# The z gates of both mixers by one Silu instead of halved product, Tanh and second product

## The chip, the cores and the metric

The kernel runs on one core of one Trainium2 chip. The metric is the device time of one execution in microseconds; the time given for a kernel is the median of its runs. The engines are called as in the profile: PE (matrix products), DVE and POOL (elementwise work), ACT (activation functions, copies, casts), SP (issues most transfers).

## The reference

One inference step of a two-layer decoder trunk for 512 prompt tokens and 8 sample tokens, which share weights; the kernel holds them side by side as 520 columns. Layer 0 is a hybrid mixer (window attention beside a Mamba-2 scan), layer 1 a gated delta net; a SwiGLU feed-forward layer follows each. In both mixers the input projection also gives a gate z, and the mixer's output is multiplied by silu(z) = z * sigmoid(z):

```python
# layer 0
y = (y + d_skip[:, None] * xs).reshape(bsz, L, SSM_D_INNER) * silu(z)
y = y * rsqrt(mean(y * y) + EPS)          # per group of 512 features
# layer 1
o = rmsnorm(o, norm_w) * silu(z.reshape(bsz, L, GDN_V_HEADS, GDN_DV))
```

The gate has 1024 features in layer 0 and 2048 in layer 1.

## The kernel before, in words

All activations lie feature-major: a tile is 128 features on the partitions by 520 token columns, which are worked in two halves of 256 and 264 columns (`HALF`). A linear layer (`lin`, line 299) holds the weights still and moves the tokens: each weight tile is split on chip into a rounded part `whi` (a cast on ACT, or on DVE) and a remainder `wlo` (a subtraction on POOL or DVE, line 165), and three products per weight tile go into a PSUM buffer `acc` for each half. There are four `acc` buffers, so two tiles of 128 features can stand in PSUM; PE cannot start a third until DVE has read the first.

The per-token norm of the layer's input is applied behind the product: the row `R2` of 520 factors multiplies the PSUM result. So a z gate needs z = acc * R2 and then silu(z). With silu(z) = (z/2) * (1 + tanh(z/2)), the kernel does this by three instructions for each half:

- a `scalar_tensor_tensor` on DVE (helper `stt`, shown as line 281): half = acc * 0.5 * R2, which also frees PSUM;
- a Tanh on ACT (helper `act`, line 284) into a scratch tile;
- a second `scalar_tensor_tensor` on DVE (line 281): (tanh + 1) * half.

Scratch comes from `tmp` (line 240), a ring of three buffers with the name `sq`, which other steps use as well.

Layer 0 (`gate_z`, line 558, called at line 649): eight z tiles, in two groups of four. The result `zt` lies in a `b` buffer (shown as `p`), and only the tanh lies in `sq`: the second product reads as `p<-sq,p`. `l0_gate` (line 861) then multiplies by the scan's output (`p<-p` or `p<-b,p`, 520 columns) and adds squares for the group's norm; `l0_norm` (line 867) takes Ln and Exp for each half, normalises and splits the result into the operands of the output projection. Ahead of that in program order are the attention of the prompt (`l0_attn`, line 936: scores, a maximum on DVE, an Exp on ACT shown as `p<-p,ast`, a reciprocal, a scaling on POOL, transposes) and of the samples (`l0_attn_sample`, line 991: eight products on POOL with the reductions of line 1011 on DVE, one Exp, then small transfers through DRAM called `pd`).

Layer 1 (`l1_gate`, line 1667, called at line 1305): sixteen z tiles. Here both the half product and the tanh lie in the `sq` ring: the second product reads as `sq<-sq`. A third product with the norm weight and the delta rule's output follows (`sq<-sq,par,Hh` or `sq<-sq,par,p`), then a cast on ACT, and a subtraction for the remainder. After the first eight tiles comes `l1_sample_state` (line 1822): for 16 pieces of the samples' states it loads a state `Hh` and a row set `ud` into one of two `cs` buffers, scales the state on POOL or DVE, adds on DVE by four `scalar_tensor_tensor` (`Hh<-cs,CS,Hh`), and stores the state. `l1_sample_gate` (line 1810) makes the sample columns of the output projection's operands (`X<-CS,p`); PE cannot finish the first tile of the output projection (`out_proj`, line 469) before.

Ahead of both gates the convolutions (`conv_tile`, line 518) also use Tanh, and the feed-forward layers use Silu already (line 1097), there with a data product on DVE ahead, a plain `tensor_tensor` (helper `tt`, shown as line 274).

The order of the instructions on each engine is laid out when the kernel is built, by a planner that takes instructions by priority (program order, or early where `high_priority` stands) as they come ready by its own durations. So work of later program lines fills gaps of earlier ones: the z tiles of layer 0 are spread among the attention's items, and the sample states of layer 1 among its z tiles. Each engine then works through its list in order. Before an activation whose function is not in the active table an ACT_TABLE_LOAD is put in; it appears in the profile under the line of the activation.

Of the kernel before, what the change touches and what calls it, by code (L numbers as in the profile page):

```python
# [121 lines left out]
def KN(n, v, *others):  # L122
    """The engine, share or order chosen at a place: v unless the table has another of the choices."""
    return KNOBS.get(n, v)
# [4 lines left out]
class WStream:  # L129
    """Weights, in the order of use: loaded in groups, split into hi + lo in units of at most 4 row tiles."""  # L130
# [38 lines left out]
    def tile(s, ap, c0, kts, spread=None, ncol=None, out=None):  # L169
        """Yield (row tile, hi, lo) for the 128 columns from c0 and the row tiles kts; input weights come two tiles a load.  # L170
        out = (buffer, offset) of 1024 floats for each four row tiles, to hold them apart from the ring."""
# [12 lines left out]
    def rows(s, ap, c0, loads):  # L184
        """As tile() for a tall matrix; loads are (first row tile, count, unit offsets in their order)."""
        for k0, n, offs in loads:
            raw = s.load(ap, k0, n, c0, 128)
            for o in offs:
                m = min(4, n - o)
                hi, lo = s.split(raw, o, m, 0)  # L190
                for j in range(m):
                    yield k0 + o + j, hi[:, j], lo[:, j]


class Ker:
# [14 lines left out]
    def gen(s, *names):  # L210
        """From here on these buffers hold something else: float32r operands and float32 data never share a tile."""
# [3 lines left out]
    def lay(s, name, off=0, n=KD, dt=F32R):  # L215
        """Operand (tile, half) -> columns, for n tiles of all tokens."""
# [3 lines left out]
    def layh(s, name, n=KD):  # L220
        """As lay(), the first half of the tokens of every tile before the second."""
        return lambda k, h: s.B(name, 256 * n * h + k * HW[h], HW[h], dt=F32R)
# [63 lines left out]
    def cp(s, e, out, in_):  # L286
        """Copy on ACT, DVE or GpSimd."""
# [10 lines left out]
    # ---- linear layers: weights stationary, 520 token columns moving in two halves  # L298
    def lin(s, w, xh, xl, nkt, halves=(0, 1), ps=None):
        """ps[half] = sum over row tiles of w (yielding (row tile, hi, lo)) of hi'xh + hi'xl + lo'xh."""  # L300
# [7 lines left out]
    def group(s, w, xh, xl, nkt):  # L308
        """Up to four tiles, the first half of the tokens of all before the second half, which may come later."""
# [13 lines left out]
    def lnexp(s, ins):  # L323
        """After ins, one table load for Ln and Exp."""
# [3 lines left out]
    def rstd(s, out, ps, n, e=EPS, keep=None, after=None):  # L328
        """out = rsqrt(ps / n + e), refined by a Newton step; keep = EPS * (ps / n + e)."""
# [17 lines left out]
    # ---- setup  # L347
# [66 lines left out]
    def add_sq(s, h, x, first, tmp, eng=None):  # L414
        """accT += x^2."""
# [7 lines left out]
    def prenorm(s, n, l, hi, lo, h, upd=None):  # L423
        """hi + lo = x * gain, exactly split."""
# [9 lines left out]
    def token_norm(s, h, keep=None):  # L434
        """s.R2 = per-token rsqrt(mean x^2 + eps), on every partition."""
# [7 lines left out]
    def boundary(s, deferred):  # L443
        """x += mp * rsqrt(mean m^2 + eps), then the next layer's prenorm (n, l, hi, lo): the second half, and the norms."""
# [5 lines left out]
    def residual(s, deferred, h):  # L450
        """One half's update of x, as a function of the feature tile."""
# [17 lines left out]
    def out_proj(s, rows, xh, xl, nkt, mp, n, l, pre, tail=2, final=False):  # L469
        """mp = m * gain, accT + sqs = sum m^2 for the eight tiles of an output projection; the last ones by token halves."""  # L470
# [46 lines left out]
    # ---- causal convolution of one 128-feature tile, then silu  # L517
# [26 lines left out]
    def conv_sample(s, nt, new, old, w, bias, out, tmp):  # L544
        """new [128, nt, 8], old [128, nt, 8, 3], w(j) [128, nt]; out [128, nt, 8] = silu(conv)."""
# [12 lines left out]
    def gate_z(s, ps, zt):  # L558
        """zt = silu(z)."""
        for h in (0, 1):  # L560
            zh = zt[:, HALF[h]]
            with s.tc.high_priority():
                s.stt(zh, ps[h], 0.5, s.R2[:, HALF[h]], ALU.mult, ALU.mult)
            tz = s.tmp(HW[h])
            s.act(tz, zh, AF.Tanh)
            s.stt(zh, tz, 1.0, zh, ALU.add, ALU.mult)

    def softplus(s, out, x, n):
        """out = max(x, 0) + log1p(exp(-|x|)); log1p(e) = 2 atanh(e / (2 + e)) as a series. Shapes [128, n]."""
# [16 lines left out]
    # ---- layer 0: input projection and mixers in the order of issue  # L586
# [78 lines left out]
    # ---- layer 0: sample convolution state  # L665
# [21 lines left out]
    # ---- layer 0: dt, decays in token layout  # L687
# [53 lines left out]
    # ---- layer 0: SSD over four chunks of 128 tokens, for one group of heads  # L741
# [78 lines left out]
    # ---- layer 0: one SSM step per sample  # L820
# [39 lines left out]
    # ---- layer 0: gate, grouped norm  # L860
# [6 lines left out]
    def l0_norm(s, g, zt, yh, yl):  # L867
        """y * silu(z) (in zt), normalised, to the exactly split yh + yl."""
# [11 lines left out]
    # ---- layer 0: attention of the prompt  # L880
# [25 lines left out]
    def l0_tokens(s, hp):  # L906
        """Keys and values token-major: the caches of the prompt and of the samples, V for the products."""
# [82 lines left out]
    # ---- layer 0: attention of the samples over their cached rows  # L990
# [67 lines left out]
    # ---- SwiGLU  # L1058
# [55 lines left out]
    def cache_shift(s):  # L1114
        """The samples' rolling caches: all rows but the oldest move up by one."""
# [11 lines left out]
    def final_early(s):  # L1127
        """x and the norm's eps of the second half token-major."""
# [27 lines left out]
    def final_first(s):  # L1156
        """The first half's outputs; m of the second half token-major, as far as it is known."""
# [26 lines left out]
    def final_last(s):  # L1184
        """The second half's outputs, token-major: x + m * rsqrt(mean m^2 + eps)."""
# [19 lines left out]
    # ---- layer 1: gated delta net, input projection and mixer in the order of issue  # L1205
# [119 lines left out]
    def vo(s, g, h, j):  # L1325
        """Half h of the tokens of v head 8 g + j: V token-major, then the outputs feature-major."""
# [5 lines left out]
    # ---- layer 1: beta, decays in token layout  # L1332
# [553 lines left out]
```

## Time and profile before

| | before |
|---|---|
| median of 3 runs | 1905.85 us |
| lowest and highest run | 1904.42, 1915.31 us |
| span of the profiled execution | 1901.6 us |
| mean granted clock of PE | 0.965 |
| z stage of layer 0 | about 263 to 364 us of the span |
| z stage of layer 1 | about 1270 to 1389 us of the span |

The profiled execution's own time is known as its span, from its first to its last instruction; the runs lie about 4 us above it. In the profile a group of instructions is shown as line, engine, operation, written tile and read tiles, shapes and count; behind the bar come the busy time in us, the mean in ns of one, and the idle time of the engine just ahead of them with what ended it. A row of the order in time is start, duration, engine, line, operation, count, and in brackets the idle time ahead. In the table by stage, each engine's busy time is followed by its count of instructions, then come the granted clock of PE, the busy share of the transfer engines and GB/s. The chain of waits is followed back from the last instruction, at each step to what released it.

### The profile page before, as it was taken

How to read it: one execution, taken by the hardware profiler on the slowest of the kernel's cores; microseconds unless marked ns; L12 is line 12 of the kernel's file. 1: busy time of each engine (PE TensorE's matmuls, PEld its weight loads, DVE VectorE, ACT ScalarE, POOL GpSimd, SP SyncE). 2: the span in 40 equal slices, each digit the busy share in tenths (PEclk: the TensorE clock that was granted, in tenths of full speed). 3: DMA queues.
4: the chain of work that ended last, by engine and by line, in shares of the span. 5: the costliest groups of instructions: out<-in, count | busy, mean ns of one | idle time of the engine just before them, and what ended most of it. 6: DMA issues, size and time to landing. Idle time of an engine off the chain costs nothing.

```text
span 1901.6 us, 36269 instructions
## 1 busy us (share of the span) xinstructions
PE 1746.8 (92%) x14263; PEld 1659.2 (87%) x14263; DVE 1190.0 (63%) x2334; ACT 748.7 (39%) x1828; POOL 876.2 (46%) x768
## 2 busy tenths in 40 slices
PE   8899999898999999988968898989889999999996
PEld 7888777698999999977857787978889899999996
DVE  6898878638323221178899977888954954443125
ACT  5432335555222223355756555544334511111222
POOL 2565756234444433435474554646668411112452
PEclk9999999998999999999988899999989899999998
DMA  7345765453333334453442123257998333432333
GB/s 259 125 130 183 237 202 142 145 182 113 111 111 112 112 106 136 124 177 114 137 139 72 59 65 92 63 156 212 272 290 237 132 135 134 134 133 84 92 92 106
DMA packets 293323, 268.88 MB, mean 141 GB/s; under 512 B 11841, under 2 KB 276742, under 8 KB 291986
## 3 DMA queue, kind: packets, MB, share of 16 engines
q1 hardware_dynamic: 292502, 265.90, 45.5%
q8 instruction: 112, 1.84, 0.4%
q10 hardware_dynamic: 652, 0.68, 0.1%
q14 instruction: 57, 0.47, 0.1%
HBM read 241.01 MB, written 62.04 MB: 159 GB/s over the span
## 4 chain that ended last, share of the span: by engine, by line
PE 56%; DVE 26%; DMA 8%; issue 4%; ACT 4%; POOL 2%; SPq 1%; DVEq 0%; POOLq 0%; ACTq 0%
PE acc L268 48%; DVE p L274 4%; DVE cs L281 4%; PE ma L268 4%; PE mb L268 3%; DVE b L274 2%; DVE sq L281 2%; DMA raw<-in_w_ffn_down_dram 2%; DVE p L281 1%; DVE Hh L281 1%; PE mb L271 1%; DVE cs L274 1%; DMA bm<-csd 1%; POOL cs L274 1%; DVE wlo L165 1%
## 5 line engine op out<-in xcount | busy, mean ns | idle before, releaser
L165 POOL TENSOR_TENSOR wlo<-raw,whi 128x512 fp32r<-128x512 f32 (+3 forms) x373 | 500.8, 1346 | 676.7 <-ACT whi L289 368.1
L268 PE MATMUL acc<-Hl,whi 128*128 128x256 f32 (+1 forms) x2576 | 565.6, 291 | 20.2 <-DVE Hl L281 8.5
L268 PEld LDWEIGHTS acc<-Hl,whi 128*128 128x128 f32 x2576 | 420.5, 193 | 35.4 <-issue 11.3
L289 ACT CAST whi<-raw 128x512 fp32r<-128x512 f32 (+3 forms) x392 | 234.4, 602 | 453.0 <-PE acc L268 388.2
L268 PE MATMUL acc<-Hh,whi 128*128 128x256 f32 (+1 forms) x1824 | 387.0, 287 | 3.5 <-DVE cs L274 2.0
L268 PE MATMUL acc<-Hh,wlo 128*128 128x256 f32 (+1 forms) x1824 | 389.0, 288 | 0.0
L268 PEld LDWEIGHTS acc<-Hh,whi 128*128 128x128 f32 x1824 | 292.5, 191 | 8.2 <-issue 5.1
L268 PEld LDWEIGHTS acc<-Hh,wlo 128*128 128x128 f32 x1824 | 292.8, 191 | 7.5 <-issue 6.7
L268 PE MATMUL acc<-bm,whi 128*128 128x256 f32 (+1 forms) x1136 | 237.1, 290 | 1.4 <-DVE bm L281 1.4
L268 PE MATMUL acc<-p,whi 128*128 128x264 f32 (+1 forms) x1280 | 230.6, 287 | 4.4 <-ACT p L1819 1.6
L290 DVE CAST whi<-raw 128x512 fp32r<-128x512 f32 x131 | 61.1, 467 | 256.7 <-PE acc L268 195.2
L165 DVE TENSOR_TENSOR wlo<-raw,whi 128x512 fp32r<-128x512 f32 (+1 forms) x150 | 117.5, 785 | 142.2 <-ACT whi L289 138.8
L268 PEld LDWEIGHTS acc<-p,whi 128*128 128x128 f32 x1280 | 190.6, 192 | 6.4 <-ACT p L1819 1.9
L268 PEld LDWEIGHTS acc<-bm,whi 128*128 128x128 f32 x1136 | 182.1, 193 | 3.7 <-issue 1.6
L268 PE MATMUL acc<-p,wlo 128*128 128x256 f32 (+1 forms) x704 | 164.4, 288 | 8.7 <-DVE wlo L165 7.0
L268 PE MATMUL acc<-Hl,wlo 128*128 128x256 f32 (+1 forms) x752 | 171.1, 293 | 1.0 <-POOL wlo L165 0.9
L268 PEld LDWEIGHTS acc<-Hl,wlo 128*128 128x128 f32 x752 | 126.4, 195 | 3.2 <-POOL wlo L165 1.6
L268 PEld LDWEIGHTS acc<-p,wlo 128*128 128x128 f32 x704 | 119.6, 192 | 10.1 <-DVE wlo L165 7.9
L281 DVE SCALAR_TENSOR_TENSOR cs<-cs,cw 128x512 f32<-128x512 f32 x100 | 96.4, 966 | 12.7 <-POOL cs L274 8.6
L268 PE MATMUL acc<-X,whi 128*128 128x264 f32 (+1 forms) x512 | 100.4, 291 | 1.7 <-DVE X L274 1.3
L268 PEld LDWEIGHTS acc<-X,whi 128*128 128x128 f32 x512 | 80.4, 195 | 3.2 <-DVE X L274 1.6
L281 DVE SCALAR_TENSOR_TENSOR Hh<-cs,CS,Hh 128x256 f32<-128x256 f32 x64 | 53.1, 894 | 26.5 <-POOL Hh L274 26.2
(465 smaller groups left out, 2932.6 us busy)
## 6 DMA issues: line engine op xcount, KB each, us to landing
raw<-in_w_gdn_in_dram SPq DMA_DIRECT2D x24, 1024.0 KB
raw<-in_w_ffn_gate_dram SPq DMA_DIRECT2D x22, 1024.0 KB
raw<-in_w_ffn_up_dram SPq DMA_DIRECT2D x22, 1024.0 KB
raw<-in_w_ffn_down_dram SPq DMA_DIRECT2D x20, 1024.0 KB
raw<-in_w_hyb_in_dram SPq DMA_DIRECT2D x16, 1024.0 KB
out_sv_dram<-in_cache_attn_v_dram SPq DMA_DIRECT2D x16, 1023.0 KB
out_sk_dram<-in_cache_attn_k_dram SPq DMA_DIRECT2D x16, 1023.0 KB
raw<-in_w_gdn_out_dram SPq DMA_DIRECT2D x10, 1024.0 KB
```

Source lines behind the costliest of these rows:

```text
L165: eng.tensor_tensor(out=lo[:, :nk, d:d + n], in0=raw[:, :, o:o + n], in1=hi[:, :nk, d:d + n].bitcast(F32), op=ALU.subtract)
L268: s.nc.tensor.matmul(out, lhsT=lhsT, rhs=rhs, start=start, stop=stop, skip_group_check=skip)
L271: s.nc.tensor.transpose(out, in_, s.ident[0:in_.shape[0], 0:in_.shape[0]])
L274: return (eng or s.nc.vector).tensor_tensor(out=out, in0=a, in1=b, op=op).ins
L281: return s.nc.vector.scalar_tensor_tensor(out=out, in0=a, scalar=sc, in1=b, op0=op0, op1=op1).ins
L289: return s.nc.scalar.copy(out, in_).ins
L290: return (s.nc.vector if e == "V" else s.nc.gpsimd).tensor_copy(out, in_).ins
```

## The change

The halving goes: DVE multiplies PSUM by `R2` alone, a Silu on ACT works in place, and the second product on DVE is not there any more. The scratch tile for the tanh goes with it, so `l1_gate` takes one buffer of the `sq` ring for a half instead of two, and `gate_z` takes none instead of one.

```diff
     def gate_z(s, ps, zt):
         for h in (0, 1):
             zh = zt[:, HALF[h]]
             with s.tc.high_priority():
-                s.stt(zh, ps[h], 0.5, s.R2[:, HALF[h]], ALU.mult, ALU.mult)
-            tz = s.tmp(HW[h])
-            s.act(tz, zh, AF.Tanh)
-            s.stt(zh, tz, 1.0, zh, ALU.add, ALU.mult)
+                s.tt(zh, ps[h], s.R2[:, HALF[h]], ALU.mult)
+            s.act(zh, zh, AF.Silu)
...
     def l1_gate(s, g, j, ps, hi, lo):
         for h in (0, 1):
             z = s.tmp(HW[h])
             with s.tc.high_priority():
-                s.stt(z, ps[h], 0.5, s.R2[:, HALF[h]], ALU.mult, ALU.mult)
-            tz = s.tmp(HW[h])
-            s.act(tz, z, AF.Tanh)
-            s.stt(z, tz, 1.0, z, ALU.add, ALU.mult)
+                s.tt(z, ps[h], s.R2[:, HALF[h]], ALU.mult)
+            s.act(z, z, AF.Silu)
```

The convolutions keep their Tanh. Comments and descriptions of functions were taken out as well, with the line numbers kept.

## Prediction

> **What bounds the kernel now.** I read the page first, for the engines' shares and the chain that ended last.
>
> ```profile
> span 1901.6 us, 36269 instructions
> PE 1746.8 (92%) x14263; PEld 1659.2 (87%) x14263; DVE 1190.0 (63%) x2334; ACT 748.7 (39%) x1828; POOL 876.2 (46%) x768
> PE 56%; DVE 26%; DMA 8%; issue 4%; ACT 4%; POOL 2%; SPq 1%; DVEq 0%; POOLq 0%; ACTq 0%
> ```
>
> PE is the bound on the whole, but a quarter of the chain is DVE's, and the change takes work from DVE. Whether it pays depends on the two places where z gates run. So I read next the table by stage: layer 0's z stage (263 to 364), its quiet middle left out, then layer 1's (1270 to 1389) in three parts.
>
> ```profile
> 263.00:328.00 65.00, 62.78 (x464) 50.87 (x463) 55.25 (x138) 32.30 (x96) 43.13 (x39) 1.00 0.63 174
> 345.00:364.00 19.00, 14.16 (x78) 9.20 (x77) 13.47 (x28) 16.14 (x31) 5.21 (x6) 0.91 0.68 226
> 1270.00:1292.00 22.00, 20.76 (x203) 15.67 (x201) 21.04 (x43) 9.52 (x23) 8.46 (x8) 1.00 0.92 259
> 1292.00:1320.00 28.00, 27.80 (x242) 24.91 (x239) 21.32 (x42) 13.33 (x28) 15.62 (x13) 1.00 0.73 211
> 1320.00:1389.00 69.00, 52.54 (x359) 49.46 (x358) 65.48 (x106) 21.68 (x52) 45.23 (x32) 0.86 0.87 247
> ```
>
> The columns are length, PE, PEld, DVE, ACT, POOL, clock, transfer share, GB/s. The last row is the one that matters: for 69 us DVE is busy 65.48 (95%) while PE has 359 products, which at the rate of the row above it (27.80 us for 242, 0.115 us each) are 41 us of work. PE is starved there, and its clock falls to 0.86. From 1292 to 1320 PE is full (27.80 of 28.00). The chain of waits inside the last part and inside layer 0's stage confirms it:
>
> ```profile
> by line: DVE sq L281 27.4%; DVE Hh L281 27.0%; DMA cs<-ud 16.9%; issue 6.7%; PE acc L268 5.6%; DVE p L274 4.4%; DVE CS L274 3.7%; DVE CS L278 3.5%; ACT p L289 1.8%; ACT sq L284 1.2%; SPq L296 1.2%; PE mb L271 0.4%; DVE X L274 0.3%; DVE acc
> ```
>
> ```profile
> by line: issue 10.4%; DVE p L281 9.7%; DMA cs<-in_state_ssm_dram 8.7%; DVE p L274 7.5%; DMA pd<-p 6.3%; DMA p<-sqd 6.1%; DVE p L1011 5.8%; PE ma L268 5.7%; POOL bm L274 4.7%; DVE wlo L165 4.4%; DVE p L957 4.1%; ACT L284 3.7%; ACT p L284 3.1
> ```
>
> In layer 1 (first row) the gate's products `sq L281` are the largest item of the chain; in layer 0 (the row below) they are about a tenth, among attention, transfers and ACT.
>
> **The change part by part.** First the product that frees PSUM. Its form changes from three operands with a constant to two operands; the feed-forward layers run the new form on the same shape.
>
> ```profile
> L281 DVE SCALAR_TENSOR_TENSOR sq<-acc,R 128x264 f32<-128x264 f32 x16 | 6.8, 424 | 0.3
> L274 DVE TENSOR_TENSOR sq<-acc,R 128x264 f32<-128x264 f32 x41 | 17.4, 423 | 0.1
> L284 ACT ACTIVATE sq<-sq 128x264 f32<-128x264 f32 x16 | 6.8, 425 | 20.0 <-DVE sq L281 19.6 <-DVE p L274 0.4
> L284 ACT ACTIVATE cs<-sq 128x264 f32<-128x264 f32 x22 | 9.3, 423 | 0.3 <-DVE sq L274 0.3
> ```
>
> 424 against 423 ns: nothing. The third row is the gate's Tanh, the fourth the feed-forward layers' Silu: 425 against 423 ns, nothing either.
>
> Second, the product (tanh + 1) * half goes: 32 instructions in layer 1, 16 in layer 0. These are its rows in layer 1 from 1320 to 1389, then in layer 0.
>
> ```profile
> L281 DVE SCALAR_TENSOR_TENSOR sq<-sq 128x264 f32<-128x264 f32 x8 | 7.3, 918 | 0.0
> L281 DVE SCALAR_TENSOR_TENSOR sq<-sq 128x256 f32<-128x256 f32 x8 | 4.2, 527 | 1.0 <-ACT sq L284 1.0
> ...
> L281 DVE SCALAR_TENSOR_TENSOR p<-sq,p 128x256 f32<-128x256 f32 x8 | 6.6, 829 | 0.0
> L281 DVE SCALAR_TENSOR_TENSOR p<-sq,p 128x264 f32<-128x264 f32 x8 | 5.6, 694 | 0.0
> ```
>
> For **layer 1's last part** that is 7.3 + 4.2 = 11.5 us off an engine that is 95% busy. The upper bound of the gain is 11.5 us, plus at most 1.0 us for the waits on ACT; the lower bound is 0, if something else holds the stretch. What is late next? PE would allow 69 - 41 = 28 us. The transfers would allow less: a share of 0.87 of 69 us is 60 us, so 9 us are left if the bytes in the stretch stay the same. Which of DVE and the transfers waits for the other is seen in SP's waits and in the sample states' row of this stretch:
>
> ```profile
> SPq L296 <- DVE Hh L281: 23.5, 6, 9.8
> ```
>
> ```profile
> L281 DVE SCALAR_TENSOR_TENSOR Hh<-cs,CS,Hh 128x256 f32<-128x256 f32 x33 | 21.4, 706 | 0.3 <-DMA cs<-ud 0.3
> ```
>
> SP waits 23.5 us for DVE to free the sample states' buffers; DVE waits 0.3 us for their rows. So the transfers follow DVE. I take 9 us, the smaller of 11.5 and the transfers' 9. In **layer 1's first parts** 16 more of these products go, but PE is busy 20.76 of 22.00 and 27.80 of 28.00 us: at most 1.4 us can come out, and I take 0.5. The smaller need of the `sq` ring (one buffer for a half instead of two) lets DVE run further ahead of ACT; its worth is inside the 1.0 us of waits above, and I take 0.
>
> For **layer 0** 6.6 + 5.6 = 12.2 us of DVE work goes, from a stretch in which DVE is busy 55.25 of 65.00 us. How much of it lies on the chain is read from the chain in order of time:
>
> ```profile
> 289.94 3.52 DVE p L281 x2
> ...
> 311.70 1.25 DVE p L281 x2
> ...
> 320.95 1.47 DVE p L281 x2
> ```
>
> These three pieces are second products: 3.52 + 1.25 + 1.47 = 6.2 us. Bounds 0 and 12.2; I take 5, as something else ready at nearly the same time will hold part of it.
>
> Third, what the change adds: **table loads on ACT**. The row of all loads at that line, then how Silu follows Exp today:
>
> ```profile
> L284 ACT ACT_TABLE_LOAD x24 | 30.8, 1283 | 7.2 <-DVE cs L281 6.0 <-DVE small L278 0.8
> ```
>
> ```profile
> 467.77 0.88 ACT L284 ACTIVATE rs<-rs 128x264 f32<-128x264 f32 x2 [0.96 <-DVE rs L278]
> 468.67 1.28 ACT L284 ACT_TABLE_LOAD   x1
> 469.96 0.42 ACT L284 ACTIVATE cs<-sq 128x256 f32<-128x256 f32 x1
> ```
>
> The pair `rs` is Ln and Exp, the last row the first Silu of the feed-forward layer: between the table with Exp used there and Silu's stands a load of 1.28 us. Tanh costs no load beside the attention's Exp: no load stands in ACT's order from 47.28 to 344.84, with both functions in use. So each change from Silu to the attention's Exp and back will cost one. ACT's order in the stage, Tanh as `sq<-p`, Exp as `p<-p,ast`, the intermediate rows left out, and as its first row the load for the convolutions' Tanh:
>
> ```profile
> 47.28 1.28 ACT L284 ACT_TABLE_LOAD   x1
> ...
> 263.40 0.77 ACT L284 ACTIVATE sq<-p 128x256 f32<-128x256 f32 x2 [1.73 <-DVE p L281]
> ...
> 273.32 0.40 ACT L284 ACTIVATE p<-p,ast 128x128 f32<-128x128 f32 x1 [3.31 <-DVE ast L278]
> ...
> 314.81 0.61 ACT L284 ACTIVATE p<-p,ast 128x384 f32<-128x384 f32 x1 [2.00 <-DVE ast L278]
> ...
> 344.84 1.28 ACT L284 ACT_TABLE_LOAD   x1
> 346.14 0.42 ACT L284 ACTIVATE rs<-rs 128x256 f32<-128x256 f32 x1
> ```
>
> The planner has spread the z tiles among the attention's items. The first six tiles each have Exps behind them before the next: six changes there and back, 12 loads; the seventh tile comes after the last Exp, one load; the eighth after the first half's Ln and Exp of the norm, one load. The loads for Ln and Exp stand there already. That is 14 loads, 14 * 1.283 = 18.0 us of ACT, which is busy 32.30 of 65.00 us in the first part. Many are covered, because a load with nothing to wait for runs while ACT idles ahead of its activation (3.31 and 2.00 us in the Exp rows above, 1.73 in the first Tanh's). What is not covered delays an Exp, and DVE's next reciprocal waits for it. Cost on the path: 0 to 18.0 us. I take two loads, 2.5 us: one before the last attention items, where z, Exp and the samples' Exp stand close together, one in the norm (345 to 364), where ACT is busy 16.14 of 19.00 us. In layer 1 the Ln and Exp of the samples' output stand between z tiles; one load for the first Silu and one behind that Exp make 2 loads, 2.6 us on an ACT busy a third of the time, covered by DVE's own work. I take 0.
>
> The Trainium skill, page "ScalarE: Activation LUTs", section "What ACT_TABLE_LOAD costs", gives 1283 ns for the load and 1380 ns for a drain with it, 2.66 us a switch. The trace has the 1283 ns, but the Ln at 346.14 starts 0.02 us after its load ends (344.84 + 1.28 = 346.12), so no drain is seen behind it. By the page, as an estimate, 16 switches would be 43 us of ACT instead of 20.5.
>
> **The sum.** -9 (layer 1's last part) - 0.5 (its first parts) - 5 + 2.5 (layer 0) = -12 us. Against the profiled span: 1901.6 - 12 = 1889.6 us. The median of the runs, 1905.85, stands 4.25 us above that span, which the change doesn't touch: 1893.9, so 1894 us, 0.6% below before.
>
> **The rivals.** *The transfers or the sample states hold layer 1.* For: the transfer share of 0.87, 16.9% of the chain there on `cs<-ud`, and the planner may put more sample states into the freed time, ahead of the output projection. Against: SP's 23.5 us of waits for DVE. Then layer 1 gives 0 and layer 0's -2.5 alone is left: 1903 us.
>
> *The table loads decide, and it becomes slower.* One mechanism, in layer 0: Silu and Exp alternate. The planner's order also may part the two halves of a tile by an Exp, which makes up to two more loads for each of seven tiles, 28 in all. Each uncovered load is 1.283 us; against them stand layer 1's 9.5 and layer 0's chain share of 6.2, so it decides from 15.7 / 1.283, 12 uncovered loads on. With 21 of 28 uncovered it is 27 - 15.7 = +11 us: 1917. For: ACT's list is in order, and DVE waits for Exp with its reciprocals. Against: ACT idles for about half of the stage, often just ahead of an Exp. The Trainium skill speaks for this rival: "ScalarE: Activation LUTs", section "Table sets: the hidden batching unit", says to batch activations by table set; by that rule 14 changes of set are the wrong trade, and the trace of before, with Tanh and Exp in one set, can't show it.
>
> *All the freed DVE time counts.* Layer 0's 12.2, layer 1's 12.5 with its waits on ACT, and 1.4 in front, no load exposed: -26 us, 1880. For: DVE pieces all along the chain, and PE's clock of 0.86, which would recover if PE were fed. Against: PE's and the transfers' own limits.
>
> *No switch at all*: the change doesn't alternate tables, because Silu stands in a set with the attention's Exp. Against: the load before the first Silu at 468.67. Then 2.5 us less: 1891.
>
> **How the numbers follow.** Forecast 0.42, transfers hold 0.20, loads decide 0.15, all counts 0.18, no switch 0.05. About 1% (19 us) is what a measurement of this kernel tells from no change. Below 1886.8 lie most of "all counts" and the edge of the forecast: 0.20. Above 1924.9 lies the far part of "loads decide": 0.07. The rest is 0.73. The forecast's own range is 1886 to 1901. The range, 1879 to 1916, takes in all the middle cases, and leaves out about half of "all counts" below and half of "loads decide" above.
>
> **What would show it.** DVE's count falls by 48, and rows `sq<-sq` and `p<-sq,p` of line 281 vanish. ACT_TABLE_LOAD rises by about 16, nearly all of it between 260 and 355 us. The stretch from 1320 to the first `X<-CS,p` shortens by 9 us with PE's clock up, and the output projection starts that much earlier. Layer 0's output projection starts about 2 us earlier. I am wrong if DVE's share in layer 1 falls and the stretch stays, if SP's waits for DVE turn into DVE's waits for `cs<-ud`, or if DVE waits for Exp in layer 0 for more than a few us in all.

## The result, and the profile after

The changed kernel takes 1922.26 us (median of 7 runs, 1917.0 to 1924.19); the kernel before, run beside it, takes 1908.32 us (median of 7, 1904.42 to 1915.31). The ratio is 1.0059, interval 1.0038 to 1.0081: about 11 us slower, where 12 us faster had been forecast. The profiled execution of the changed kernel took 1917.0 us, with a span of 1915.2 us and a mean granted clock of 0.96.

From its page the span, the engines' busy times and the chain by engine:

```profile
span 1915.2 us, 36236 instructions
...
PE 1754.5 (92%) x14263; PEld 1665.0 (87%) x14263; DVE 1156.6 (60%) x2286; ACT 778.8 (41%) x1851; POOL 870.0 (45%) x768
...
PE 56%; DVE 18%; DMA 5%; ACT 5%; issue 3%; POOL 1%; SPq 0%; DVEq 0%; ACTq 0%; POOLq 0%
```

DVE lost 48 instructions (2334 to 2286) and 33.4 us of work, and its share of the chain fell from 26% to 18%. So the relief that the change was priced for is there. ACT gained 23 instructions and 30.1 us. The span grew all the same.

The groups of the gate, by form:

```profile
L274 DVE TENSOR_TENSOR sq<-acc,R 128x264 f32<-128x264 f32 x57 | 24.1, 423 | 0.1
L274 DVE TENSOR_TENSOR p<-acc,R 128x264 f32<-128x264 f32 x16 | 6.7, 418 | 0.0
L284 ACT ACTIVATE sq<-sq 128x264 f32<-128x264 f32 x16 | 6.8, 423 | 0.0
L284 ACT ACT_TABLE_LOAD x47 | 60.3, 1283 | 12.6 <-DVE cs L281 6.1 <-DVE ast L278 5.0 <-DVE small L278 0.8
```

Each instruction costs what it was priced at: the product 423 and 418 ns, the Silu 423 ns. ACT_TABLE_LOAD went from 24 to 47 at this line: 23 more, where 16 were forecast, at 1283 ns each. Their idle time ahead has a new item, 5.0 us ended by `ast`, which is the operand of the attention's Exp.

Where the span was lost is seen from a landmark that occurs once in each layer's output projection, a table load at line 500. In the order of time, first before, then after:

```profile
419.26 1.28 ACT L500 ACT_TABLE_LOAD   x1
814.15 1.28 ACT L500 ACT_TABLE_LOAD   x1
1467.35 1.28 ACT L500 ACT_TABLE_LOAD   x1
1863.91 1.28 ACT L500 ACT_TABLE_LOAD   x1
```

```profile
427.58 1.28 ACT L500 ACT_TABLE_LOAD   x1
822.06 1.28 ACT L500 ACT_TABLE_LOAD   x1
1479.74 1.28 ACT L500 ACT_TABLE_LOAD   x1
1876.34 1.28 ACT L500 ACT_TABLE_LOAD   x1
```

Layer 0 ends 8.3 us later. The first feed-forward layer takes 394.9 and 394.5 us, the last one 396.6 both times: nothing there. Between the second and the third landmark lies layer 1: 653.2 us before, 657.7 us after, 4.5 us more, where 9.5 us less were forecast. So both places have to be explained.

**Layer 0.** The table loads of this stage (258 to 368 us) alone, before and then after:

```profile
L284 ACT ACT_TABLE_LOAD x4 | 5.1, 1283 | 0.1
```

```profile
L284 ACT ACT_TABLE_LOAD x22 | 28.2, 1283 | 5.4 <-DVE ast L278 5.0
```

18 loads were added here. How they lie is seen in ACT's order after (start, duration; idle time ahead in brackets). Silu is `p<-p` with 256 or 264 columns, the attention's Exp `p<-p,ast`:

```profile
267.95 0.27 ACT L289 COPY p<-mb 128x128 f32<-128x128 f32 x1 [2.39 <-PE mb L268]
272.07 1.28 ACT L284 ACT_TABLE_LOAD   x1 [3.85 <-DVE ast L278]
273.36 0.40 ACT L284 ACTIVATE p<-p,ast 128x128 f32<-128x128 f32 x1
...
274.38 1.28 ACT L284 ACT_TABLE_LOAD   x1
275.68 0.42 ACT L284 ACTIVATE p<-p 128x256 f32<-128x256 f32 x1
276.11 1.28 ACT L284 ACT_TABLE_LOAD   x1
277.41 0.40 ACT L284 ACTIVATE p<-p,ast 128x128 f32<-128x128 f32 x1
...
277.92 1.28 ACT L284 ACT_TABLE_LOAD   x1
279.21 0.42 ACT L284 ACTIVATE p<-p 128x264 f32<-128x264 f32 x1
```

Two things are to be seen. ACT idles 3.85 us for the Exp's operand, and only then does the table load run: the wait stands ahead of the load, not between load and Exp, so the idle time covers nothing of it. Of the 22 loads this holds for two (272.07 and 312.58, with 1.15 us); nearly all the others stand directly behind other work, and their activation follows at once. And the two halves of one z tile (256 and 264 columns) are parted by an Exp, with four loads within six us. DVE's waits for ACT in the stage (us in total, times, longest), before and then after:

```profile
DVE ast L961 <- ACT p L284: 2.3, 5, 0.9
```

```profile
DVE ast L959 <- ACT p L284: 11.0, 12, 2.3
DVE p L274 <- ACT p L284: 6.0, 5, 1.6
```

The first is the reciprocal that waits for Exp: 2.3 us became 11.0. The second is the gating product, which now waits for Silu. In the chain of waits of 263 to 374 us the loads are the second largest item (line 284 without a tile is a table load), 12.7% of 111 us, 14 us, where before had 3.7% of 101 us:

```profile
by line: PE acc L268 24.9%; ACT L284 12.7%; PE ma L268 12.3%; DMA cs<-in_state_ssm_dram 8.1%; PE mb L268 5.6%; issue 5.3%; ACT p L284 4.3%; PE mb L271 3.9%; ACT rs L284 2.7%; DVE p L281 2.4%; DVE p L274 2.4%; DMA p<-pd 2.1%; DVE rs L281 2.1
```

**Layer 1.** The stretch of the sample states, from the first `Hh<-cs,CS,Hh` to `X<-CS,p`, before and then after:

```profile
1327.65 4.34 DVE L281 SCALAR_TENSOR_TENSOR Hh<-cs,CS,Hh 128x256 f32<-128x256 f32 x4
...
1388.35 0.21 DVE L274 TENSOR_TENSOR X<-CS,p 128x64 fp32r<-128x64 f32 x1
```

```profile
1352.50 3.17 DVE L281 SCALAR_TENSOR_TENSOR Hh<-cs,CS,Hh 128x256 f32<-128x256 f32 x4
...
1399.76 1.91 DVE L274 TENSOR_TENSOR X<-CS,p 128x64 fp32r<-128x64 f32 x1
```

60.7 us became 47.3: 13.4 us shorter, more than the 9 forecast. But it begins 24.9 us later. 7.9 us of that were there when layer 1 began (the second landmark above), 8.9 at 1060.2 us (the 300th weight split of the next section, 1069.2 us after), so 16 us were lost between there and this stretch; 6.6 of them already by 1240.6 us (the next section's 320th weight split, 15.5 us later there), in the scans, where hardly any z gate runs. That was not in the prediction at all.

### The profile page after: what moved, and what is told of

Same layout as the page of the kernel before. It is cut to its first block, busy times and chain, and to the rows that moved or that the text cites. A ratio compares the mean times of both kernels' runs of the same rounds, so it can differ in the third digit from the quotient of the medians.

```text
span 1915.2 us, 36236 instructions
## 1 busy us (share of the span) xinstructions
PE 1754.5 (92%) x14263; PEld 1665.0 (87%) x14263; DVE 1156.6 (60%) x2286; ACT 778.8 (41%) x1851; POOL 870.0 (45%) x768
## 4 chain that ended last, share of the span: by engine, by line
PE 56%; DVE 18%; DMA 5%; ACT 5%; issue 3%; POOL 1%; SPq 0%; DVEq 0%; ACTq 0%; POOLq 0%
PE acc L268 48%; PE ma L268 4%; DVE p L274 3%; PE mb L268 3%; DVE cs L281 2%; DVE b L274 1%; ACT L284 1%; DMA raw<-in_w_ffn_down_dram 1%; PE mb L271 1%; DVE p L1455 1%; DVE Hh L281 1%; DVE Hh L274 1%; ACT p L284 1%; DVE cs L274 1%; DVE Hl L281 1%
## 5 line engine op out<-in xcount | busy, mean ns | idle before, releaser
L165 POOL TENSOR_TENSOR wlo<-raw,whi 128x512 fp32r<-128x512 f32 (+3 forms) x373 | 495.7, 1333 | 690.3 <-ACT whi L289 393.5
L268 PE MATMUL acc<-Hh,wlo 128*128 128x256 f32 (+1 forms) x1824 | 390.3, 289 | 0.0
L268 PEld LDWEIGHTS acc<-p,wlo 128*128 128x128 f32 x704 | 119.3, 193 | 11.7 <-DVE wlo L165 7.6
L281 DVE SCALAR_TENSOR_TENSOR cs<-cs,cw 128x512 f32<-128x512 f32 x100 | 94.3, 945 | 11.8 <-POOL cs L274 7.7
```

The costliest lines, as they stand in the source:

```text
L165: eng.tensor_tensor(out=lo[:, :nk, d:d + n], in0=raw[:, :, o:o + n], in1=hi[:, :nk, d:d + n].bitcast(F32), op=ALU.subtract)
L268: s.nc.tensor.matmul(out, lhsT=lhsT, rhs=rhs, start=start, stop=stop, skip_group_check=skip)
L281: return s.nc.vector.scalar_tensor_tensor(out=out, in0=a, scalar=sc, in1=b, op0=op0, op1=op1).ins
```

## The experiments

To compare stages I use the subtractions that make the weights' remainders (line 165; `wlo<-raw,whi`, ten of them into other tiles). Every trace has 533 of them, in the same sequence of layers. Counted from 0, the 48th starts at about 220 us, shortly before layer 0's z tiles, the 108th at 463 us behind that layer's mixer, the 300th at 1060 us, 246 us into layer 1 but 160 us ahead of its first z product, the 372nd at 1455 us as its output projection runs. The differences of their start times are the lengths of the stages, so "108 to 300" holds the first feed-forward layer and the first part of layer 1; for the changed kernel these starts are 219.5, 471.3, 1069.2 and 1467.4 us. They come from one profiled execution each, and stages with the same code and order differ by up to 5 us; the ratios come from several runs on one chip. "Order of layer 1" says whether SP issues layer 1's transfers in the sequence of the kernel before (with the new gate, up to the z gates, where e4, e9, e10, e12 and e16 agree with each other). The "other" sequences agree with each other up to the z gates as well, but for one transfer of e15. The column speaks of SP alone: DVE's and ACT's orders in e9, e10, e12, e14 and e16 are not those of before.

| kernel | ratio, interval | median us | table loads | layer 0, 48 to 108 | 108 to 300 | layer 1, 300 to 372 | order of layer 1 |
|---|---|---|---|---|---|---|---|
| before | | 1905.85 | 30 | 242.7 | 597.0 | 394.8 | before's |
| after | 1.0059 (1.0038 to 1.0081) | 1922.26 | 53 | 251.8 | 597.8 | 398.3 | other |
| e1 Tanh alone | 1.0012 (0.9999 to 1.0025) | 1908.22 | 30 | 236.8 | 598.0 | 398.0 | other |
| e2 Silu, product kept | 1.0046 (1.0030 to 1.0063) | 1914.72 | 50 | 244.2 | 595.2 | 400.8 | before's |
| e3 layer 0 only | 1.0095 (1.0071 to 1.0118) | 1923.13 | 48 | 253.7 | 597.9 | 403.1 | other |
| e4 layer 1 only | 0.9977 (0.9964 to 0.9990) | 1901.61 | 35 | 245.7 | 595.4 | 390.3 | before's |
| e5 Silu held | 0.9992 (0.9977 to 1.0007) | 1907.56 | 35 | 235.4 | 598.9 | 399.2 | other |
| e6 one Silu a tile | 1.0006 (0.9993 to 1.0019) | 1909.77 | 49 | 245.6 | 597.0 | 398.0 | a third |
| e7 conv state first | 1.0081 (1.0059 to 1.0102) | 1926.44 | 53 | 250.1 | 597.0 | 398.9 | forced |
| e8 held, conv first | 1.0000 (0.9986 to 1.0013) | 1909.67 | 35 | 238.6 | 598.3 | 400.0 | forced |
| e9 held, knob | 0.9972 (0.9959 to 0.9986) | 1905.69 | 37 | 240.0 | 598.8 | 390.3 | before's |
| e10 change, knob | 1.0007 (0.9995 to 1.0019) | 1912.14 | 48 | 248.4 | 597.1 | 392.9 | before's |
| e11 before, knob | 1.0019 (1.0006 to 1.0033) | 1915.42 | 30 | 242.7 | 597.1 | 404.7 | other |
| e12 held, knob | 0.9965 (0.9952 to 0.9978) | 1903.60 | 35 | 241.6 | 600.8 | 391.6 | before's |
| e13 before again | 1.0004 (0.9991 to 1.0016) | 1910.78 | 30 | 242.5 | 599.1 | 398.0 | before's |
| e14 before, knob | 1.0003 (0.9988 to 1.0018) | 1911.61 | 30 | 242.0 | 599.2 | 399.2 | before's |
| e15 before, knob | 1.0062 (1.0038 to 1.0085) | 1921.25 | 30 | 247.3 | 599.4 | 405.5 | other |
| e16 change, knob | 1.0012 (0.9997 to 1.0027) | 1912.16 | 50 | 250.0 | 599.5 | 395.3 | before's |

The kernel before, run beside them, took 1906.3 us with e1 to e4, 1909.5 us with e5 to e8, 1911.0 us with e9 to e12 and 1910.75 us with e13 to e16; so across these groups the ratios are to be compared.

### Which part of the edit costs: e1 to e4

e1 takes the changed kernel and swaps its function. The instructions on PE, DVE, POOL and SP are the same and in the same order; only the added loads are missing:

```diff
-            s.act(zh, zh, AF.Silu)
+            s.act(zh, zh, AF.Tanh)
...
-            s.act(z, z, AF.Silu)
+            s.act(z, z, AF.Tanh)
```

> The changed kernel with Tanh written where it has Silu: the gate is tanh(z) and not silu(z), so part of the computation is another one. Every engine's order is that of the changed kernel, and only the 23 table loads that came with Silu are gone. Theory A (the loads cost the time): the 8.1 us lost in layer 0's z stage vanish and turn into the gain of 2 to 6 us that the removed DVE products are worth there; layer 1 gains as well; 1890 to 1902 us in all, 15 to 25 us under the changed kernel. Theory B (the planner's new order costs the time, the loads are covered): it stays within 4 us of the changed kernel, 1915 to 1922 us, with layer 0 still 6 to 8 us late.

e2 is the other half: the kernel before with both products, Silu in place of Tanh, and so the order of before with 20 loads more:

```diff
-            s.act(tz, zh, AF.Tanh)
+            s.act(tz, zh, AF.Silu)
...
-            s.act(tz, z, AF.Tanh)
+            s.act(tz, z, AF.Silu)
```

> The kernel before with Silu written where its z gates have Tanh, and the second DVE product kept: the gate is (silu(z/2) + 1) * z/2, so part of the computation is another one. Every engine's order is that of before, with 20 more table loads. Theory A: layer 0's stage is 8 to 15 us longer, layer 1 up to 3 us; 1915 to 1925 us. Theory B: within 4 us of before, 1905 to 1912 us. Together with the run before it this makes a square of four: product kept or not, loads or not.

e3 has the change in `gate_z` alone, e4 in `l1_gate` alone.

> The change in layer 0's gate alone. If the two layers are independent: layer 0 ends 8 us later, everything behind it keeps that, 1914 to 1918 us. If the new order that layer 0's change gives to layer 1 made the loss of some 7 us in layer 1's scans, that loss shows here too, and it is 1918 to 1926 us.

> The change in layer 1's gate alone. Prediction's term for it: 9.5 us faster, 1897 to 1901 us. If layer 1's own change brings the 7 us lost in the scans and the part given back in the z stage, as in the whole change: about 4 us slower, 1910 to 1914 us.

In layer 0 the loads decide. Without them (e1) the stage is 236.8 us, with them (after, e3) 251.8 and 253.7: about 15 us for 18 loads, 65% of their 23.1 us. The order can't make this difference, since it is the same in e1 and in the changed kernel. In the time of the whole program the loads cost less than their stage shows, or about as much: 9 us against e1, 13 against e5 below, 15 for e7 against e8, each with an interval of about 5 us either way. e1 as a whole (1908.22 us) lies between the ranges of both theories: theory A had layer 1 gain, and at 398.0 us it didn't. DVE's waits for Exp, in e1 over 260 to 368 us, are back near before's:

```profile
DVE ast L959 <- ACT p L284: 3.9, 7, 0.9
```

The surprise is e2: 14 loads more in the order of before, and the stage stays at 244.2 us, within the scatter of the unedited stages (242.7, 245.7 and 242.5). Part of the reason can be counted, because e1 is the changed order and before the order of e2, both without the added loads. In before, ACT idles directly ahead of 11 of the 14 activations that get a load in e2; with at most one load's length counted for each, that could cover 9.7 of 18.0 us. In e1 it idles ahead of 6 of the 18 that get one in the changed kernel: 5.6 of 23.1 us. The two halves of one tile among the Exps, in e1 (with Tanh in Silu's place), show how close they stand:

```profile
319.57 0.72 ACT L284 ACTIVATE p<-p,ast 128x512 f32<-128x512 f32 x1
...
320.29 0.40 ACT L284 ACTIVATE p<-p 128x256 f32<-128x256 f32 x1
320.60 0.71 ACT L284 ACTIVATE p<-p,ast 128x512 f32<-128x512 f32 x1
...
321.31 0.41 ACT L284 ACTIVATE p<-p 128x264 f32<-128x264 f32 x1
```

The changed kernel has a load ahead of each of the last three. That what stays uncovered in e2 hides behind DVE's second products, which are gone in the changed kernel, is a reading that no run shows. Nor were e2's loads free: its time is 0.46% above before, 8.8 us. Its one profile has 1.5 us of that in layer 0's stage and 6.0 in layer 1 (400.8 us), where six loads were added in before's own order; the same stage of before varied by 3.2 us.

e4 is faster than before by 0.23%, e3 slower by 0.95%. And e3, in which layer 1's z code is that of before, has a layer 1 of 403.1 us, 8 us longer than before. Something of layer 0's edit reaches layer 1, although the feed-forward layer between them stays as it was (394.1 us between the landmarks for 394.9).

### Taking the loads away another way: e5 and e6

e5 keeps the whole change, but queues layer 0's Silus behind the last Exp of both attentions:

```diff
-            s.act(zh, zh, AF.Silu)
+            with s.tc.issue_after(s.last_exp), s.tc.issue_after(s.last_exp_s):
+                s.act(zh, zh, AF.Silu)
```

> The whole change, but layer 0's Silus are queued on ACT behind the attention's last Exps (prompt and samples), so that Silu and Exp alternate no more: 35 table loads in the program instead of 53, 7 of them in layer 0 instead of 25. Theory A (the loads on the relieved order's chain cost layer 0 about 15 us): layer 0 (from the 48th to the 108th weight split) gains 2 to 6 us on before instead of losing 9; with layer 1's own gain of 4.7 the time is 1896 to 1900 if layer 1's scans keep before's order, about 1907 if they still lose 8 us. Rival B (not the loads but the reordering itself, or the gate coming late, costs layer 0): layer 0 still loses 5 us or more, and the time is 1915 or above.

e6 makes one Silu of the two halves, so that an Exp can't stand between them:

```diff
-            s.act(zh, zh, AF.Silu)
+        s.act(zt, zt, AF.Silu)
```

> The whole change, but layer 0's gate is one Silu over the 520 columns of a tile, so that no Exp can part a tile's halves: 49 table loads instead of 53, 14 added in layer 0 instead of 18. Theory A1 (each load that parts halves is a full 1.283 us on the chain, the others cost what they cost before): 4 loads, 5 us off layer 0's loss of 9, time about 1917. Theory A2 (the parted halves are what makes the loads exposed): layer 0 comes near the relief of -6 plus the 2 us that the loads cost in the old order, loss gone, about 1910. Rival B (number of loads does not matter, the order does): 1922 as the change itself, or worse because the second half's gate waits for the first.

e5 gives the 15 us of layer 0 back and a little more (235.4 us), and theory A stands; the time, 1907.56 us, is the case "layer 1's scans still lose". In e6 only four loads are gone, but 6 us of layer 0's stage (251.8 to 245.6): about 1.5 us for each, which would make the loads that part a tile the dearest; with one profile, a scatter of up to 5 us and eight Silus fewer in e6 that is not shown. The 14 left cost the rest, 245.6 - 236.8 = 9 us, while the 14 loads of e2, in the order of before, leave layer 0's stage as it was. Layer 0 fits A1 (5 us expected) better than A2 (loss gone); the time, some 10 us lower by the ratios (1.0059 to 1.0006), is better than A1 gave, for which one profile of each does not account.

### What happens in layer 1: e7 and e8

In the changed kernel SP's first store of the convolution state comes 26.4 us behind the first load of it (1168.34 to 1194.70 us), in before 18.1 us (1154.74 to 1172.88). I took this for the cause, and gave the state's code priority in the whole change (e7) and in e5 (e8):

```diff
-        s.l1_conv_state()
+        with s.tc.high_priority():
+            s.l1_conv_state()
```

> The whole change, but layer 1's sample convolution state is issued with priority, ahead of the scans' work, where the change's order has it about 11 us later than before's. Theory C (its late transfers, on which PE, ACT and DVE wait inside the scans, make layer 1's loss of 8 us that layer 0's edit causes): layer 1 (from the 300th to the 372nd weight split) goes from +3.5 to about -4, time about 1914. Rival D (the late conv state is a by-product, and the scans lose the time by another order of PE and DVE): layer 1 stays at +3 to +4, time 1920 to 1924. Layer 0 stays at +9 in both.

> Both of the last edits together: layer 0's Silus behind the attention's last Exps, and layer 1's sample convolution state with priority. Theories A and C both right: layer 0 -2 to -6, layer 1 -4 to -5, time 1894 to 1899, better than both kernels. Only A right: as the kernel with the held Silus. Only C right: about 1914.

Theory C falls. The first store comes earlier, 20.4 us behind the first load in e7, but layer 1 stays at 398.9 and 400.0 us, and neither kernel is faster than the one it was made from.

### The order alone: e9 to e16

The next idea was that it isn't one transfer. The planner lays out the instructions by its own durations; an edit in layer 0 shifts its clock, and layer 1's work comes out in another sequence. To test it without touching layer 1, I turned knobs of layer 0 that have nothing to do with the gate, and chose them by the sequence that layer 1 gets. e9 is e5, e10 the whole change, each with another share of the z weights' remainders on POOL (`lp_z0`: none, a half; else a third). e12 is e5 with the copies of the attention's values on DVE instead of ACT (`vals`). All three bring before's sequence back. e11 is the kernel before with half of the attention's transposed items copied by DVE instead of ACT (`turn0`), which gives it the other sequence.

```diff
 # e9 and e10
+ 'lp_z0': 0,
+ 'lp_z0': 2,
 # e11 and e12
+ 'turn0': 'V',
+ 'vals': 'V',
```

> The whole change with layer 0's held Silus, and one knob of layer 0 (the share of the z weights' remainders that GpSimd splits: none instead of a third), chosen because with it the planner issues layer 1's transfers in the same order as in the kernel before; layer 1's code is that of the change. Theory E (layer 1's loss of about 8 us is nothing that the new gate costs, but another order into which the planner tips when layer 0's timing shifts): layer 1 (300th to 372nd weight split) goes from +4 to about -4.7, as where only layer 1 was changed; with layer 0 at -3 to -7 the time is 1894 to 1900. Rival F (layer 1 loses for another reason that layer 0's edit brings, whatever the order): layer 1 stays at +4, time 1905 to 1910.

> The whole change as it is (Silu alternating with Exp), and the same knob with all but half of the remainders' splits moved (a half on GpSimd instead of a third): with it, too, layer 1's transfers are in the order of the kernel before. 48 table loads instead of 53. Theory E: layer 1 at about -4.7 instead of +3.5; layer 0 still loses, +5 to +9 for its loads; time 1908 to 1914. Rival F: layer 1 at +3 to +4, time 1916 to 1922.

> The kernel before without any part of the change, but one knob of layer 0 turned (the copies of half of the attention's transposed items on VectorE instead of ScalarE), chosen because the planner then issues layer 1's transfers in the order that it has where only layer 0's gate is changed. Theory E: layer 1 loses about 8 us without any Silu in the kernel; with layer 0's own few us for the knob the time is 1912 to 1920. Rival F: layer 1 stays within 2 us of before, time 1903 to 1912.

> As the first of these, with another knob that brings layer 1's order of before: the copies of the attention's values on VectorE instead of ScalarE. Theory E: layer 1 at about -4.7 again, layer 0 at 0 to -7 by what the knob does to VectorE, time 1894 to 1903. Rival F: layer 1 at +4, time 1905 or above.

Layer 1 follows the sequence each time: 390.3, 392.9 and 391.6 us with before's, 404.7 with the other and the old gate. In time, e9 is 5.7 us above what theory E gave, in rival F's range, and e12 is 0.6 us above; but the kernel before is 5 us higher on this chip as well (1911.0 us for 1905.85). But e11's time moved by 0.19% alone, 3.6 us where the stage showed 9.9, and before's profile was from an earlier occasion with a median 5 us lower. So before itself was profiled again on e11's chip (e13); e14 and e15 are before with one knob at two values, a half and a quarter of the remainders on POOL, of which the second tips layer 1; and e16 gives the whole change the knob of e11, which in that kernel brings before's sequence back.

```diff
 # e14 and e15
+ 'lp_z0': 2,
+ 'lp_z0': 4,
 # e16
+ 'turn0': 'V',
```

> The kernel before, unchanged, profiled on the chip of the next three. Both theories: ratio 1.000, and layer 1 (300th to 372nd weight split) 394 to 396 us long, layer 0's stage (48th to 108th) 242 to 246.

> The kernel before, with half instead of a third of the z weights' remainders of layer 0 split on GpSimd: the planner keeps layer 1's order. Theory E (order alone): layer 1 394 to 396 us, time within 0.2% of before. Rival F (what reaches layer 1 is not the order): no prediction of its own here; it is the control for the next run.

> The same with a quarter instead of a third: the planner gives layer 1 the other order, that of the change with held Silus. No part of the change is in the kernel. Theory E: layer 1 403 to 405 us, time 0.3 to 0.5% above before. Rival F: layer 1 394 to 397, time as in the run with the half.

> The whole change as it is, with the knob that cost the kernel before layer 1's order (copies of half of the attention's transposed items on VectorE): here it brings before's order of layer 1 back. 50 table loads. Theory E: layer 1 390 to 393 us instead of 398, layer 0 still 248 to 252 for its loads; time 0 to 0.3% above before, that is 6 to 10 us below the change. Rival F: layer 1 398 to 400, time 0.4 to 0.7% above before.

Before's layer 1 is 398.0 us long on this chip, 3 us more than in the first profile: expectations built on 394.8 missed by as much. The difference is what counts. e14 and e15 have the same code in layer 1 and no part of the change, and their landmarks on either side of it are, first e14, then e15 (line numbers are one higher, for the knob's own line):

```profile
812.34 1.28 ACT L501 ACT_TABLE_LOAD   x1
1472.28 1.28 ACT L501 ACT_TABLE_LOAD   x1
```

```profile
820.06 1.28 ACT L501 ACT_TABLE_LOAD   x1
1486.55 1.28 ACT L501 ACT_TABLE_LOAD   x1
```

659.9 us became 666.5. What differs is in SP's list; the loads of layer 1's sample convolution state and its first store, e14, then e15:

```profile
1154.26 0.50 SPq L297 DMA_DIRECT2D ex<-in_state_gdn_conv_dram  x1
1157.97 1.52 SPq L297 DMA_DIRECT2D b<-gqd  x2
1159.96 0.33 SPq L297 DMA_DIRECT2D ex<-in_state_gdn_conv_dram  x1
...
1174.23 0.26 SPq L297 DMA_DIRECT2D out_pgc_dram<-ex  x1
```

```profile
1163.34 0.50 SPq L297 DMA_DIRECT2D ex<-in_state_gdn_conv_dram  x1
1168.86 0.33 SPq L297 DMA_DIRECT2D b<-gqd  x1
1169.41 0.32 SPq L297 DMA_DIRECT2D ex<-in_state_gdn_conv_dram  x1
1170.80 0.33 SPq L297 DMA_DIRECT2D b<-gqd  x1
...
1195.11 0.28 SPq L297 DMA_DIRECT2D out_pgc_dram<-ex  x1
```

From the first load to the first store it is 20.0 us in e14 and 31.8 in e15: the two loads of `b<-gqd` that stand together in e14 are spread. The time of e15 is 0.62% above before (of 11.8 us some 5 are layer 0's, for the knob). And the same knob that costs the kernel before 0.19% takes the change from 1.0059 to 1.0012. e16's layer 1, 395.3 us, lies between what theory E (390 to 393) and rival F (398 to 400) gave. Put together, by gate and sequence, the layer-1 lengths of these executions add up (e1 and e2 left out, whose gates are neither of the two; e2, with 400.8 us in before's sequence, would be the highest of its cell):

| | before's sequence | other sequences |
|---|---|---|
| old gate | 394.8, 398.0, 399.2; mean 397.3 | 403.1, 404.7, 405.5; mean 404.4 |
| new gate | 390.3, 390.3, 391.6, 392.9, 395.3; mean 392.1 | 398.0, 398.3, 398.9, 399.2, 400.0; mean 398.9 |

The new gate is worth 5 us in layer 1 in either column, and the sequence costs 7 us in either row. On one chip alone (e9 to e16), the sequence costs the old gate 6.5 us and the new gate is worth 6.1. That is theory E; rival F, by which the loss would come from layer 0's edit whatever the sequence, falls with e9, e10, e12 and e16. What inside the scans takes the 7 us was not settled: e7 shows that it isn't the late store alone. Nor is it known which of the planner's choices tips.

e4, e9 and e12 are faster than both kernels: 0.23%, 0.28% and 0.35% below before, each with an interval that ends below 1.

## Why the prediction was wrong, step by step

- *The product, the Silu and the removed products.* Right: 423 and 418 ns for 424, 423 for 425, 48 instructions of DVE less.
- *Layer 0's relief, -5 us.* Right: without loads the stage is 236.8, 235.4 and 238.6 us (e1, e5, e8) against 242.7, 242.5 and 245.7 unedited, 6.7 us less in the mean.
- *The table loads in layer 0, "I take two loads, 2.5 us".* This step failed, by its size: they cost 15 us (251.9 us, the mean of after, e3 and e7, against 236.9 without). The count of 14 was right for the order of before (e2 has 14 more); it became 18 because the new order parts the halves of two tiles by an Exp, two loads more for each. Worse was the cover: "a load with nothing to wait for runs while ACT idles ahead of its activation". Loads do run so in before, here with 6.37 us of idle time left behind the load:

```profile
985.63 1.28 ACT L284 ACT_TABLE_LOAD   x1
993.29 0.22 ACT L284 ACTIVATE small<-small 128x16 f32<-128x16 f32 x1 [6.37 <-DVE small L278]
```

  Of the idle times that the prediction named, the first Tanh's 1.73 us was used so (the load at 259.90, with 0.44 us left), but at the Exps the load stood behind the wait (272.07, after 3.85 us, and 312.58, after 1.15 us). The trace holds what tells them apart: all four loads of the changed kernel that idle time stands ahead of, but for the program's first, come 0.03 us behind a separate waiting instruction (EVENT_SEMAPHORE, which the rows don't list; it ends at 272.04 and 312.55 here). The rest is that idle time was counted as a sum: by e1, 5.6 of 23.1 us could be covered in the new order, and even in before's 9.7 of 18.0. What the prediction named as its refutation is there: DVE waits 11.0 us for Exp.
- *The rival "the table loads decide".* This is what happened in layer 0. It gave 12 uncovered loads as the point from which it decides; 15 us are worth 11.7, so by its own sum the time would have stayed as it was. That its 1917 us lies near the measured time is in part luck: what makes it slower is layer 1's sequence (7 us) and its smaller gain (5 for 9.5 us), which this rival doesn't have. It had a chance of 0.15. The Trainium skill, page "ScalarE: Activation LUTs", section "Table sets: the hidden batching unit", tells to batch activations by table set. The runs here agree: batched (e5), 35 loads instead of 53, ratio 0.9992 instead of 1.0059.
- *Layer 1's last part, -9 us, and its first parts, -0.5 us.* The last part gave 13.4 us, more than the bound of 12.5, but not as a gain: in e4, where nothing else is changed, it is 13.7 us shorter (1336.46 to 1383.49 us), because it begins 8.8 us later and ends only 4.9 earlier. The sample products that come before it are spread over more time there, 29.7 us from first to last in before and 33.7 in e4, first before's rows, then e4's:

```profile
1273.90 0.47 DVE L281 SCALAR_TENSOR_TENSOR ex<-mb,cst,ex 128x256 f32<-128x256 f32 x1
...
1303.55 0.48 DVE L281 SCALAR_TENSOR_TENSOR ex<-mb,cst,ex 128x256 f32<-128x256 f32 x1 [1.39 <-PE mb L268]
```

```profile
1276.94 0.47 DVE L281 SCALAR_TENSOR_TENSOR ex<-mb,cst,ex 128x256 f32<-128x256 f32 x1
...
1310.60 0.48 DVE L281 SCALAR_TENSOR_TENSOR ex<-mb,cst,ex 128x256 f32<-128x256 f32 x1 [0.74 <-PE mb L268]
```

  Over layer 1 as a whole 5 us are left of the forecast 9.5. The sign was right; the length of one stretch was taken for the gain of the layer.
- *The other rivals.* Transfers didn't take DVE's place in layer 1: over 1345 to 1401 us SP still waits for DVE to free the sample states' buffers, 21.5 us where it had been 23.5:

```profile
SPq L296 <- DVE Hh L281: 21.5, 5, 11.5
```

  "No switch" fell with the 23 loads, "all counts" with layer 0.
- *Layer 1's loads, 2 at no cost.* Five were added; the cost is right for the new order: e1 without them has a layer 1 of 398.0 us, after with them 398.3. In before's order (e2, six loads) it is open.
- *Layer 1 ahead of the gate.* No step dealt with it: the sum held the stretch from 1060 to 1270 us for unchanged, because hardly an edited line runs there. Layer 1 lost 7 us by another sequence of the planner; what loses them inside the scans is open.

Summed with the measured sizes: -6.7 + 15.0 in layer 0, -5.2 + 6.8 in layer 1, +9.9 us, against 11.3 by the ratio (0.0059 of 1908.32). The same sum fits e1 less well: without the loads it gives -5 us, and e1 is 2 us slower than before, so each of these sizes may be off by some us. With before's sequence in layer 1 and the loads held off (e9, e12), two of the four terms are left, and the kernel is faster, as the forecast of -12 us had it by sign but at half its size.

## What to carry to other kernels

Before swapping an activation function, list ACT's order with its table sets: count every change of set, with halves and interleaved items, and price each at the full load, less the idle time that stands directly ahead of that one activation, and nothing less where the trace has a load of that kind behind the wait. Loads that idle time would cover in the old order can stand uncovered in the order that the edit brings, so the relief and the loads must not be summed as if they were independent. Where a planner lays out the program, an edit can cost as much in a layer that it doesn't touch as it gains where it acts: compare stage by stage, hold the order fixed in a control, and turn an unrelated knob of the kernel before to learn how far its time moves by the order alone.

## What was not expected of the hardware

Of the 23 table loads on ACT between 258 and 368 us of the changed kernel (22 at line 284, one at 326), 21 are followed by their instruction within 0.02 us, and the two others by idle times of 0.44 and 0.95 us; 5.0 us of idle time stand ahead of two loads instead, ended by the operand of the activation behind. Over the whole program the first case is no rarer: in before, the program's first load left out, 17.0 us of idle time stand behind eight loads and 6.8 us ahead of two. No cost beyond the 1283 ns is seen: the load at 272.07 ends at 273.35, and Exp starts at 273.36. The Trainium skill, page "ScalarE: Activation LUTs", section "What ACT_TABLE_LOAD costs", gives a drain of 1380 ns besides; in this trace it doesn't show.
